# Feed-forward products in two-by-two blocks with seven products for eight, in a decoder layer on one core

## The chip, the core and the metric

The kernel runs on one core of a Trainium2 chip, as one launch. The metric is the device time of that launch in microseconds (us). The engines are PE (TensorE: matmuls and the loads of their stationary operand), DVE (VectorE), ACT (ScalarE), POOL (GpSimd) and SP (SyncE, which here only issues DMAs). Matmuls write to PSUM; all other data is in SBUF, 128 partitions wide.

## What is computed

One layer over 528 tokens (512 of the input behind 16 learned ones), model width 1024, hidden width 2816, all in float32:

```python
def swiglu_ffn(h, w_gu, w_down):
    gate, up = jnp.split(h @ w_gu, 2, axis=-1)
    return (jax.nn.silu(gate) * up) @ w_down

h = h + 0.5 * swiglu_ffn(rms_norm(h, ffn1_norm), ffn1_w_gu, ffn1_w_down)
h = h + hybrid_mixer(rms_norm(h, mix_norm), w_in, conv_w, b_f, ...)
h = h + 0.5 * swiglu_ffn(rms_norm(h, ffn2_norm), ffn2_w_gu, ffn2_w_down)
return rms_norm(h[:, 16:], final_norm)
```

The mixer (a short gated convolution beside an attention with forget gates) is the same in both kernels. The two feed-forward networks hold most of the arithmetic: 1024 x 5632 weights for gate and up, 2816 x 1024 for down, each.

## The kernel before

Activations lie transposed, with features on partitions and tokens as columns: hT is 8 tiles of [128, 528]. A weight tile of 128 x 128 is the stationary operand of a matmul and the tokens are the moving one. To keep float32's precision at float32r's speed, each operand is split into two float32r parts, hi and lo, and each product is made of three matmuls: hi x hi, hi x lo, lo x hi (mm, L281). Splitting costs one ACT cast for hi (L78) and one DVE subtraction for lo (L79).

The class Weights streams the weights in the order of use: SP loads run two loads ahead (L57), and units of [128, 8, 128] are split three units ahead. The first network works in chunks of 8, 8 and 6 of the 22 hidden tiles of 128. For each hidden tile the gate product runs over 8 tiles of the model width, then the up product, then ACT and DVE make silu(gate) x up and split it into hid_h and hid_l (gate, L299 to L306; up, L312 to L319). After each chunk the down products of the 8 output tiles run over the chunk's hidden tiles and DVE adds them to hT (L322). Its 528 columns are two matmuls of 264 in two PSUM banks. The second network does the same with 512 columns in one bank, chunks of 8, 8 and 4, and a last chunk of 2 whose down product has the tokens on partitions, so that the final norm can begin per tile of tokens. The gain of the norm is on the operand (L239, L244), and 1/rms is multiplied onto the product.

The start is written out by hand: the first three products of the first network run side by side while the input arrives, tile by tile. Elsewhere a scheduler sets the order of the instructions on each engine, and Weights.done and take place the splits between the products. POOL does some memsets, the sums of squares at the start (L254) and the small DMAs of the attention's forget gates (L544, L553).

Of the kernel before, what the change touches and what calls it, by code (L numbers as in the profile page):

```python
# [14 lines left out]
P = 128  # L15
D = 1024
# [17 lines left out]
class Weights:  # L34
    """Streams weight units [128, k, 128]: loads run ahead, then each unit is split
    into two float32r parts hi + lo, which together hold every bit of the float32."""

    def __init__(self, nc, raw_pool, pool, ahead, loads_ahead):
        self.nc, self.raw_pool, self.pool = nc, raw_pool, pool
        self.ahead, self.loads_ahead = ahead, loads_ahead  # L40
        self.loads, self.units = [], []
        self.raw, self.ready = {}, {}
        self.n_loaded = self.n_ready = self.n_used = 0
# [8 lines left out]
    def load(self, whole=True):  # L52
        ap, nk, cols = self.loads[self.n_loaded]
        t = self.raw_pool.tile([P, 2048], F32, name="raw")
        v = t[:, : nk * cols].rearrange("p (k c) -> p k c", c=cols)
        if whole:
            self.nc.sync.dma_start(out=v, in_=ap)  # L57
# [6 lines left out]
    def open(self, pool=None):  # L64
        """Takes the next unit's two tiles; split_slice fills them."""
        pool = pool or self.pool
        hi = pool.tile([P, 8, P], F32R, name="w_hi")
        lo = pool.tile([P, 8, P], F32R, name="w_lo")
# [11 lines left out]

    def split(self):
        load, _, nk, cols = self.units[self.n_ready]
        while self.n_loaded < len(self.loads) and self.n_loaded <= load + self.loads_ahead:
            self.load()
# [10 lines left out]
    def take(self, i=0):  # L95
        self.fill()
        return self.ready[self.n_used + i]

    def done(self):
        del self.ready[self.n_used]  # L100
        self.n_used += 1
        self.fill()


class Acc:
    """A product in PSUM: in one bank, or in the halves of its columns in two banks.
    Columns are named by position (0..L)."""
# [6 lines left out]
    def each(self, f):  # L114
        """f(psum view, g) for as few views as hold the product; g cuts an operand alike."""
# [9 lines left out]
def layer(ctx, tc, x, meta, n1, gu1, dn1, nm, w_in, conv_w, b_f, g_conv, g_attn, w_out, n2, gu2, dn2, nf, out):  # L125
# [751 lines left out]
```

## Time and profile before

| | us |
|---|---|
| three runs, median | 1015.25 |
| lowest, highest | 1014.94, 1017.09 |
| span of the profiled execution | 1013.3 |
| PE busy | 998.2 |
| DVE busy | 516.9 |
| ACT busy | 382.1 |
| POOL busy | 43.0 |

The span is from the first to the last instruction; what the runs' time has beyond it lies around the program. The page gives busy time by engine, then the chain of work that ended last, followed back from the last instruction to what released each step. Groups of instructions are named by line, engine, operation and tiles (out<-in). Matmuls are pipelined, so the duration of one is longer than the distance between two starts. The first network lasts until about 401 us, the mixer until about 641, the second network until about 993, and the rest is the final norm and the output.

### The profile page before, as it was taken

The page shows a single profiled execution, that of the slowest core. Times are in us where ns is not written, and L with a number is a line of the kernel's source. Part 1 is how long each engine was busy: PE and PEld are TensorE (multiplying, and loading weights), DVE is VectorE, ACT ScalarE, POOL GpSimd, SP SyncE. Part 2 cuts the span into 40 slices and gives each one's busy share as a digit, 9 for nine tenths or more (in the row PEclk, how much of TensorE's full clock was granted, in tenths as well). Part 3 has the DMA queues.
Part 4 walks back from the last instruction along what each step waited for, and adds up shares of the span by engine and source line. Part 5 has one row for each costly group of instructions (what it writes and reads, how often), then busy time and mean ns, then how long its engine had stood idle before and what let it go on. Part 6 is the DMA issues. An engine that isn't in the chain of part 4 may idle for free.

```text
span 1013.3 us, 14940 instructions
## 1 busy us (share of the span) xinstructions
PE 998.2 (99%) x6338; PEld 906.6 (89%) x6338; DVE 516.9 (51%) x787; ACT 382.1 (38%) x612; POOL 43.0 (4%) x76
## 2 busy tenths in 40 slices
PE   9999999999999999999999999999999999999996
PEld 8999999999999999989899888888888888888884
DVE  6844333444334446676766657644433444334445
ACT  5622212222122244675656665523222232222335
POOL 4100000000000002200000000100000000000002
PEclk9999999999999999999999999999999999999998
DMA  6422222223223212232233122323332223231312
GB/s 211 160 91 84 84 83 84 83 84 126 83 84 93 86 53 72 77 104 66 63 83 95 58 83 84 104 94 114 102 105 83 83 84 125 84 104 41 107 40 84
DMA packets 102707, 91.99 MB, mean 91 GB/s; under 512 B 3604, under 2 KB 101056, under 8 KB 102640
## 3 DMA queue, kind: packets, MB, share of 16 engines
q1 hardware_dynamic: 101792, 90.42, 28.4%
q8 instruction: 50, 0.82, 0.4%
q10 hardware_dynamic: 144, 0.52, 0.1%
q0 software_dynamic: 704, 0.09, 0.1%
q14 instruction: 17, 0.14, 0.0%
HBM read 88.86 MB, written 2.10 MB: 90 GB/s over the span
## 4 chain that ended last, share of the span: by engine, by line
PE 92%; ACT 3%; DVE 3%; issue 1%; DMA 0%; SPq 0%; DVEq 0%; ACTq 0%
PE bank L281 50%; PE acc L281 37%; PE bank L712 2%; PE bank L679 1%; PE bank L643 1%; DVE w_lo L79 1%; ACT w_hi L78 0%; DVE sm L650 0%; DMA raw<-in_ffn_w_gu_dram 0%; ACT sm L153 0%; DVE hT L389 0%; PE bank L514 0%; ACT sm L664 0%; ACT xh L239 0%; PE bank L802 0%
## 5 line engine op out<-in xcount | busy, mean ns | idle before, releaser
L78 ACT CAST w_hi<-raw 128x1024 fp32r<-128x1024 f32 (+5 forms) x184 | 175.5, 958 | 550.5 <-PE bank L281 218.3
L79 DVE TENSOR_TENSOR w_lo<-raw,w_hi 128x1024 fp32r<-128x1024 f32 (+4 forms) x183 | 208.2, 1141 | 43.6 <-ACT w_hi L78 40.3
L281 PE MATMUL bank<-xl,w_hi 128*128 128x512 f32 (+2 forms) x672 | 216.1, 353 | 0.0
L281 PE MATMUL bank<-xh,w_hi 128*128 128x512 f32 (+2 forms) x672 | 216.1, 352 | 0.0
L281 PE MATMUL bank<-xh,w_lo 128*128 128x512 f32 (+2 forms) x672 | 215.4, 352 | 0.0
L281 PE MATMUL acc<-xh,w_hi 128*128 128x264 f32 x704 | 141.7, 286 | 1.7 <-ACT xh L239 1.3
L281 PE MATMUL acc<-xh,w_lo 128*128 128x264 f32 x704 | 142.0, 287 | 0.0
L281 PE MATMUL acc<-xl,w_hi 128*128 128x264 f32 x704 | 140.6, 284 | 0.3 <-DVE xl L244 0.3
L281 PEld LDWEIGHTS bank<-xh,w_hi 128*128 128x128 f32 x672 | 118.1, 188 | 18.8
L281 PEld LDWEIGHTS bank<-xh,w_lo 128*128 128x128 f32 x672 | 117.9, 188 | 17.8
L281 PEld LDWEIGHTS bank<-xl,w_hi 128*128 128x128 f32 x672 | 117.7, 188 | 17.8
L281 PEld LDWEIGHTS acc<-xh,w_hi 128*128 128x128 f32 x704 | 109.5, 190 | 2.2 <-ACT xh L239 1.6
L281 PEld LDWEIGHTS acc<-xh,w_lo 128*128 128x128 f32 x704 | 109.0, 190 | 0.0
L281 PEld LDWEIGHTS acc<-xl,w_hi 128*128 128x128 f32 x704 | 107.6, 188 | 0.5 <-DVE xl L244 0.5
L281 PE MATMUL acc<-hid_h,w_hi 128*128 128x264 f32 x352 | 71.7, 285 | 0.0
L281 PE MATMUL acc<-hid_l,w_hi 128*128 128x264 f32 x352 | 71.7, 285 | 0.0
L281 PE MATMUL acc<-hid_h,w_lo 128*128 128x264 f32 x352 | 71.6, 285 | 0.0
L281 PE MATMUL bank<-hid_h,w_hi 128*128 128x512 f32 x160 | 62.9, 393 | 0.0
L281 PE MATMUL bank<-hid_h,w_lo 128*128 128x512 f32 x160 | 62.4, 390 | 0.0
L281 PE MATMUL bank<-hid_l,w_hi 128*128 128x512 f32 x160 | 62.4, 390 | 0.0
L281 PEld LDWEIGHTS acc<-hid_h,w_hi 128*128 128x128 f32 x352 | 54.7, 188 | 0.0
L281 PEld LDWEIGHTS acc<-hid_l,w_hi 128*128 128x128 f32 x352 | 54.5, 188 | 0.0
(233 smaller groups left out, 1061.7 us busy)
## 6 DMA issues: line engine op xcount, KB each, us to landing
raw<-in_ffn_w_gu_dram SPq DMA_DIRECT2D x42, 1024.0 KB, 5.0
raw<-in_ffn_w_down_dram SPq DMA_DIRECT2D x16, 1024.0 KB, 5.2
raw<-in_w_in_dram SPq DMA_DIRECT2D x24, 512.0 KB, 4.0
raw<-in_ffn_w_down_dram SPq DMA_DIRECT2D x4, 768.0 KB, 4.6
raw<-in_ffn_w_down_dram SPq DMA_DIRECT2D x6, 512.0 KB, 3.7
raw<-in_w_out_dram SPq DMA_DIRECT2D x3, 896.0 KB, 5.1
raw<-in_ffn_w_gu_dram SPq DMA_DIRECT2D x8, 256.0 KB, 6.4
out_dram<-ob SPq DMA_DIRECT2D x8, 256.0 KB, 2.2
```

Source lines behind the costliest of these rows:

```text
L78: nc.scalar.copy(h, src)
L79: nc.vector.tensor_sub(lw, src, h.bitcast(F32))
L281: nc.tensor.matmul(ap, lhsT=wt[:, kw, :], rhs=mt[:, k, c0 - off:c1 - off], start=(first and a == 0 and b == 0), stop=(last and a == len(ks ...
L643: nc.tensor.matmul(t[:, o:o + c1 - c0], lhsT=qt[:, i * P:(i + 1) * P], rhs=kt[:, c0:c1], start=(b == 0), stop=(b == 1))
L679: nc.tensor.transpose(o, sm[:, SOFF[i] + j * P:SOFF[i] + (j + 1) * P], ident)
L712: nc.tensor.matmul(oo, lhsT=lt, rhs=rt, start=(a == 0 and n_ == 0), stop=(a == 1 and n_ == len(ops) - 1))
```

## The change

The products of both networks are cut into blocks of two by two by two: two tiles of the output (gate and up of one hidden tile, or two output tiles of down), pairs of tiles of the inner dimension, and two halves of the token columns (264 each in the first network, 256 in the second). With blocks A of the weights and B of the activations, the seven products are A11 B11, A12 B21, and five of sums of blocks, in Winograd's form of Strassen's scheme. A unit of seven products runs over 4 pairs of inner tiles for gate and up, and over 3 or 2 pairs of hidden tiles for down. Gate and up of the first 6 hidden tiles of the first network and the first 4 of the second stay as they were ("classical"), and so does the down product of the last 2 hidden tiles of the second network.

The activations of each pair of tiles are kept in seven forms, each split into hi and lo: three are blocks and four are sums of blocks, which POOL makes (L379 to L386). They lie in one arena of float32r with the operands of the mixer. Of the four sums of weight blocks, two are made by a DMA that POOL issues and that adds to what SP has loaded before (L474, L478), two by DVE (L486, L489). Each of the four groups of weights (nat, s24, ss, 22) is then cast by ACT (L499) and subtracted by DVE (L503). Where several outputs share a partial result, ACT copies it from one bank to the next with its sign turned (L546, L547), and a fifth bank holds the one product that two outputs take from SBUF.

Work in the networks is now placed by hand in slots, one product each: Slots.at puts a task behind slot t, on whatever engine it runs. `b` is a unit's first slot; the next unit's is b + 7.

```diff
+        def pair_forms(self, r, s0, s1, t0, t1):
...
+            def sums1():
+                t = ts["t"]
+                b12, b21, b22 = self.half(s0(), 1), self.half(s1(), 0), self.half(s1(), 1)
+                nc.gpsimd.tensor_add(t[:, 1], t[:, 0], b22)
+                nc.gpsimd.tensor_sub(t[:, 2], b12, b22)
+                nc.gpsimd.tensor_sub(t[:, 3], b21, t[:, 1])
...
+        def prep(self, b, nat, base, acc, a22, nj):
+            def load():
+                raw["nat"] = self.pool_raw.tile([P, 8, P], F32, name="raw")
+                nc.sync.dma_start(out=raw["nat"][:, :2 * nj], in_=nat)
+                raw["ss"] = self.pool.tile([P, 2, nj, P], F32, name="ss", tag="ss", bufs=2)
+                for i in range(2):
+                    nc.sync.dma_start(out=raw["ss"][:, i], in_=base[i])
+            def add():
+                for i in range(2):
+                    nc.gpsimd.dma_start(out=raw["ss"][:, i], in_=acc[i], accum_op=ALU.add)
+            def s2():
+                raw["s24"] = self.pool.tile([P, 2, nj, P], F32, name="s24")
+                nc.vector.tensor_add(raw["s24"][:, 0], raw["ss"][:, 1], raw["nat"][:, 0:2 * nj:2])
+            def s4():
+                nc.vector.tensor_add(raw["s24"][:, 1], raw["s24"][:, 0], raw["nat"][:, 1:2 * nj:2])
...
+            sl.at(b - 13, load, 3)
+            sl.at(b - 9, add, 3)
+            sl.at(b - 7, load22, 3)
+            sl.at(b - 4, s2, 3)
+            sl.at(b - 3, s4, 3)
+            for nm_, t in (("nat", b - 3), ("s24", b - 1), ("ss", b), ("22", b + 2)):
+                sl.at(t, lambda nm_=nm_: hi(nm_), 3)
+                sl.at(t + 1, lambda nm_=nm_: lo(nm_), 3)
...
+        def products(self, nj, rhs, w):
+            b = sl.slot(prod(A, "nat", lambda j: 2 * j, F_B11, True))
+            sl.slot(self.p4)
+            sl.slot(prod(A, "nat", lambda j: 2 * j + 1, F_B21, False))
+            sl.slot(prod(B, "s24", lambda j: j, F_T2, False))
+            sl.slot(prod(E, "ss", lambda j: nj + j, F_T1, True))
+            sl.slot(prod(B, "ss", lambda j: j, F_T3, False))
+            sl.slot(prod(C, "s24", lambda j: nj + j, F_B22, False))
+            self.p4 = prod(B, "22", lambda j: j, F_T4, False)
...
+            sl.at(b + 1, lambda: nc.scalar.activation(B, A, AF.Copy, scale=-1.0), 0)
+            sl.at(b + 4, lambda: nc.scalar.activation(C, B, AF.Copy, scale=-1.0), 0)
+            sl.at(b + 5, copy_e, 0)
...
+        def down(self, j0, nj, m):
+            sl.at(b + 3, add(h00, A), 0)
+            sl.at(b + 6, add(h11, B), 0)
+            sl.at(b + 6, lambda: nc.gpsimd.tensor_sub(h11, h11, self.e5), 0)
+            sl.at(b + 7, add(h01, C), 0)
+            sl.at(b + 7, lambda: nc.gpsimd.tensor_add(h01, h01, self.e5), 0)
+            sl.at(b + 9, add(h10, B), 0)
...
+            g_units(range(14, NF))
+            for m in range(0, ND, 2):
+                F.down(6, 2, m)
+            for m in range(0, ND, 2):
+                for i, t in enumerate(F.down(8, 3, m)):
+                    def fin(d=m + i):
+                        operand(d, GMIX, L, xm)
+                        squares(d, L, nc.gpsimd)
+                    sl.at(t, fin, 1)
```

In the first network down runs over hidden pairs 0 to 2, 3 to 5, 6 and 7, and 8 to 10; in the second over 0 to 2, 3 to 5, 6 and 7, and 8 and 9. The gain, 1/rms and the half of the residual are now on the forms of the operand and on the hidden tiles, and the output is finished in hT in place of a buffer of its own.

DVE in the first network, one hidden tile, before (w_lo is a weight's low part, s and hd the gate and the product with up):

```order
L299 SCALAR_TENSOR_TENSOR s<-acc,rs 128x528
L79 TENSOR_TENSOR w_lo<-raw,w_hi 128x1024
L306 SCALAR_TENSOR_TENSOR s<-s,rs 128x528
L312 TENSOR_TENSOR hd<-acc,s 128x528
L79 TENSOR_TENSOR w_lo<-raw,w_hi 128x1024
L319 TENSOR_TENSOR hid_l<-hd,hid_h 128x528
```

The same engine and place now (s_1814 and s_1941 are sums of weight blocks, e_1845 the shared product, r_1765 the block A22):

```order
L489 TENSOR_TENSOR s_1814<-s_1814,raw 128x512
L503 TENSOR_TENSOR w_lo<-raw,w_hi 128x1024
L572 TENSOR_TENSOR hd<-acc,e_1845 128x264
L575 TENSOR_TENSOR s<-acc,e_1845 128x264
L503 TENSOR_TENSOR w_lo<-s_1814,w_hi 128x1024
L503 TENSOR_TENSOR w_lo<-ss,w_hi 128x1024
L579 SCALAR_TENSOR_TENSOR hd<-acc,s 128x264
L580 SCALAR_TENSOR_TENSOR hd<-hd,s 128x264
L503 TENSOR_TENSOR w_lo<-r_1765,w_hi 128x512
L486 TENSOR_TENSOR s_1941<-ss,raw 128x512
L371 TENSOR_TENSOR arena<-hd,arena 128x264
```

A hidden tile has four low parts in place of two, two sums of weights, and the next unit's first sum stands between this unit's evacuations and the forms of its hidden tile.

POOL from the start's sums of squares through the whole first network to the mixer, before:

```order
L378 AFFINE_SELECT mask<-mask 128x128
L254 TENSOR_TENSOR ssum<-ssum,sq 128x528 x7
L87 MEMSET w_hi 128x1024
L493 MEMSET q2a 64x512
L493 MEMSET k2a 64x528
```

POOL within the down units of the second group of hidden pairs now (ss receives the accumulating DMAs, e_2604 and e_2707 are shared products):

```order
L478 DMA ss<-in_ffn_w_down_dram 128x3x128 x2
L384 TENSOR_TENSOR ts<-ts,hd 128x264
L385 TENSOR_TENSOR ts<-hd 128x264
L386 TENSOR_TENSOR ts<-hd,ts 128x264
L478 DMA ss<-in_ffn_w_down_dram 128x3x128 x2
L606 TENSOR_TENSOR hT<-hT,e_2604 128x264
L608 TENSOR_TENSOR hT<-hT,e_2604 128x264
L478 DMA ss<-in_ffn_w_down_dram 128x3x128 x2
L606 TENSOR_TENSOR hT<-hT,e_2707 128x264
L608 TENSOR_TENSOR hT<-hT,e_2707 128x264
```

Where POOL had nothing between the sums of squares and the memset of the mixer's first weights, it now has two accumulating DMAs per unit, and the forms' sums or two corrections of hT stand between one pair and the next.

ACT where the start hands over to the third hidden tile of the first network, before (y and tt are steps of 1/rms):

```order
L153 ACTIVATE y_492<-y_492 128x264
L145 ACT_TABLE_LOAD
L260 ACTIVATE tt<-y_492 128x264
L153 ACTIVATE raw<-raw 128x528 x2
L317 CAST hid_h<-raw 128x528
L78 CAST w_hi<-raw 128x1024
```

And now:

```order
L191 ACTIVATE y_482<-y_482 128x264
L183 ACT_TABLE_LOAD
L294 ACTIVATE tt<-y_482 128x264
L455 CAST w_hi<-raw 128x1024
L191 ACTIVATE raw<-raw 128x528 x2
L455 CAST w_hi<-raw 128x1024
```

The first cast that stands here now is that of the third hidden tile's own gate weights; before, these were cast ahead of the steps of 1/rms, and the one shown is for a later tile.

## Rows read from the trace of the kernel before

**Rows 1.** The page: busy time by engine, and the last chain's shares by engine.

```profile
PE 998.2 (99%) x6338; PEld 906.6 (89%) x6338; DVE 516.9 (51%) x787; ACT 382.1 (38%) x612; POOL 43.0 (4%) x76
...
PE 92%; ACT 3%; DVE 3%; issue 1%; DMA 0%; SPq 0%; DVEq 0%; ACTq 0%
```

**Rows 2.** The chain in order of time: start us, us, what; the two networks.

```profile
38.24 362.72 PE acc L281 x2976
...
641.37 308.94 PE bank L281 x1341
```

**Rows 3.** Busy time by stretch: PE, PEld, DVE, ACT, POOL, clock, DMA share, GB/s.

```profile
38.20:401.00 362.80, 362.80 (x2978) 362.79 (x2978) 157.76 (x190) 99.22 (x125) 1.12 (x2) 1.00 0.28 88
...
500.00:600.00 100.00, 98.58 (x637) 89.37 (x636) 68.33 (x155) 61.70 (x123) 3.57 (x10) 1.00 0.25 76
...
641.00:950.00 309.00, 309.00 (x1343) 251.80 (x1342) 132.73 (x156) 82.03 (x101) 2.20 (x1) 1.00 0.28 92
```

**Rows 4.** Timeline of PE (start us, us): 258 columns, then 512.

```profile
476.22 0.40 PE L281 MATMUL bank<-xh,w_hi 128*128 128x258 f32 x2
...
476.94 0.28 PE L281 MATMUL bank<-xh,w_hi 128*128 128x258 f32 x1
...
699.81 0.40 PE L281 MATMUL bank<-xl,w_hi 128*128 128x512 f32 x1
...
710.93 0.40 PE L281 MATMUL bank<-xl,w_hi 128*128 128x512 f32 x1
```

**Rows 5.** Groups by form: busy us, mean ns | idle before them, releasers.

```profile
L79 DVE TENSOR_TENSOR w_lo<-raw,w_hi 128x1024 fp32r<-128x1024 f32 x145 | 177.6, 1225 | 37.0 <-ACT w_hi L78 33.9 <-PE bank L281 0.6
...
L78 ACT CAST w_hi<-raw 128x1024 fp32r<-128x1024 f32 x145 | 152.1, 1051 | 494.4 <-PE bank L281 194.0 <-PE acc L281 170.1 <-issue 127.2
...
L244 DVE SCALAR_TENSOR_TENSOR xl<-hT,gains,xh 128x528 fp32r<-128x528 f32 x16 | 12.2, 766 | 4.7 <-ACT xh L239 4.6
...
L79 DVE TENSOR_TENSOR w_lo<-raw,w_hi 128x768 fp32r<-128x768 f32 x8 | 7.7, 959 | 0.0
...
L79 DVE TENSOR_TENSOR w_lo<-raw,w_hi 128x512 fp32r<-128x512 f32 x8 | 5.4, 681 | 0.0
...
L695 DVE TENSOR_TENSOR l<-bank,h 128x384 fp32r<-128x384 f32 x8 | 4.4, 549 | 0.0
...
L551 DVE SCALAR_TENSOR_TENSOR ks<-bank,rs 128x264 f32<-128x264 f32 x8 | 3.3, 424 | 0.4 <-PE bank L281 0.4
```

**Rows 6.** DVE beside POOL: two timeline rows, then line 79 and two groups.

```profile
21.38 1.31 POOL L254 TENSOR_TENSOR ssum<-ssum,sq 128x528 f32<-128x528 f32 x1 [0.87 <-ACT sq L253]
...
21.56 1.41 DVE L79 TENSOR_TENSOR w_lo<-raw,w_hi 128x256 fp32r<-128x256 f32 x1
...
L79 DVE TENSOR_TENSOR w_lo<-raw,w_hi x22: 407/696/1553, 6.5 to 56.8; 128x256 fp32r<-128x256 f32 x16, 128x1024 fp32r<-128x1024 f32 x6
...
L79 DVE TENSOR_TENSOR w_lo<-raw,w_hi 128x256 fp32r<-128x256 f32 x16 | 11.0, 713 | 0.1
...
L254 POOL TENSOR_TENSOR ssum<-ssum,sq 128x528 f32<-128x528 f32 x7 | 9.5, 1357 | 16.4 <-ACT sq L253 16.3
```

**Rows 7.** DMA issues (KB, us to landing), a POOL issue, an SP issue.

```profile
raw<-in_ffn_w_down_dram SPq DMA_DIRECT2D x6, 512.0 KB, 3.7
...
xc<-in_x_dram SPq DMA_DIRECT2D x2, 256.0 KB, 3.2
...
bf<-in_b_f_dram POOLq DMA_DIRECT2D x1, 0.0 KB, 4.8
...
L544 POOL DMA_DIRECT2D q2a<-fr x4 | 2.2, 554 | 20.8 <-DVE fr L536 16.1 <-PE bank L643 4.7
...
204.39 0.37 SPq L57 DMA_DIRECT2D raw<-in_ffn_w_gu_dram  x1
```

**Rows 8.** Timeline of DVE where the start hands over to the network.

```profile
34.42 2.36 DVE L79 TENSOR_TENSOR w_lo<-raw,w_hi 128x1024 fp32r<-128x1024 f32 x2 [0.24 <-ACT w_hi L78]
...
39.23 0.43 DVE L261 SCALAR_TENSOR_TENSOR tt<-sm,tt 128x264 f32<-128x264 f32 x1 [0.76 <-ACT tt L260]
```

More of the change, by code (lines that the diff above doesn't have):

```diff
@@ L321, in down @@
[L321 to L340 removed]
+    F_B11, F_B21, F_B22, F_T1, F_T2, F_T3, F_T4 = range(7)
@@ L443, in layer @@
             nc.vector.tensor_copy(gains[:, 8:], gp[:, :36])
+            nc.vector.tensor_scalar(ghalf, gains[:, :24], -0.5, None, ALU.mult)
             table(SILU_SET)
-        with tc.tile_pool(name="hid1", bufs=2, reuse_waits="tile") as hid1:
-            for ci, (_, nf_) in enumerate(CHUNKS1):
-                hh, hl = hidden(hid1, L)
-                gate_up(new1, nf_, hh, hl, 0, start=[*accs, a3] if ci == 0 else None)
-                for m in range(ND):
-                    acc = new1()
-                    mm(acc, W.take(), range(nf_), hh, hl)
-                    down(acc, m)
-                    if ci == len(CHUNKS1) - 1:
-                        operand(m, GMIX, L)
-                        squares(m, L)
-                    W.done()
+        for _ in range(4):
+            W.done(False)
@@ L515, in layer @@
         sa = new(L)
[L516 removed]
+        row_sums(sa, *split2(ssum, L))
         W.done()
@@ new lines, in tokens, with gain_row @@
+                nc.scalar.copy(hT[:, m, NM:], bank_x)
+            done = []
+            for m in range(0, ND, 2):
+                done += F.down(8, 2, m)
+            g_units(range(NF - N_LAST, NF))
+            F.end()
+            for m, t in enumerate(done):
+                sl.add(t + 2, lambda m=m: tokens(m))
+            t_gb = done[0]
+            def gain_row():
+                v["gb"] = pool.tile([P, 4, 256], F32, name="ts").rearrange("p a c -> p (a c)")
+                nc.scalar.dma_start(out=v["gb"], in_=nf.rearrange("(o d) -> o d", o=1).broadcast_to([P, D]))
@@ new lines, in layer, with obs @@
+            W.done(False)
+            for k in range(NF - N_LAST, NF):
+                add_row(dn2, k)
+            sl.at(n - 16, W.prefetch, 4)
+            for i in range(N_LAST):
+                sl.at(n - 4 + 3 * i, W.split, 4)
+            sl.run()
+        table(EXP_SET)
+        hh, hlo = hl
+        gb = v["gb"]
+        ws = [W.take(i) for i in range(N_LAST)]
+        pss = bk[0] + bk[2] + [bank_x, bank_e] + bk[1]
+        def obs(i, b):
+            return hT[:, 4 * b:4 * b + 4, NM + i * P:NM + (i + 1) * P]
```

593 lines of the change are left out of this document (406 added, 187 removed).

## Prediction, made before the changed kernel ran

> **What bounds the kernel now.** I read the page first: PE is busy 99% of the span, and the chain that ended last runs on PE for 92% of it [rows 1]. The chain in order of time then shows where: one unbroken piece of 362.72 us in the first feed-forward network and one of 308.94 us in the second [rows 2]. In the same two stretches DVE is busy 157.76 of 362.80 us (43%) and 132.73 of 309 us (43%), ACT 27%, POOL hardly, the DMA engines 28%, and the granted clock is full [rows 3]. So PE alone sets the time there, and fewer matmul columns shorten the kernel as long as nobody else becomes late. The profiled execution has a span of 1013.3 us; the median of the runs is 1015.25, so 1.95 us lie around the span, and I keep them.
>
> **What PE saves.** A matmul of 264 columns takes 0.1219 us of the unbroken piece (362.72 / 2976 [rows 2]). One of 512 columns starts every 0.2317 us (48 between 699.81 and 710.93 [rows 4]). The change cuts the first network from 3168 to 2844 matmuls of 264 columns: 324 x 0.1219 = 39.5 us. In the second network 1344 matmuls of 512 columns (18 gate/up tiles x 48, 480 in the down products) become 2352 of 256. Nearest to 256 columns are the 258-column ones of the mixer: six starts in 0.72 us, 0.120 each [rows 4]; the line through 264 and 512 columns gives 0.118. I take 0.119: 1344 x 0.2317 - 2352 x 0.119 = 311.4 - 279.9 = 31.5 us (33.4 at 0.118, 29.2 at 0.120). Together 71.0 us.
>
> The Trainium skill ("TensorE: Matmul & The Clock Gate", Back-to-back issue gap) gives 262 cycles for 256 columns at full clock, which is 0.109 us. The rows at 258 and 264 columns lie 0.01 us above its formula, and those at 512 by 0.016; by that page of the Trainium skill the second network would save another 23 us, and as the rows contradict it I give this no chance.
>
> **What the other engines get instead.** The two networks now hold 66 units of seven products: 34 gate/up units (84 matmuls, 10.2 us of PE in the first network), 20 down units over three pairs of hidden tiles (63, 7.7 us) and 12 over two pairs (42; 5.12 us in the first network, 5.00 in the second). Each unit splits four groups of weights (1024, 1024, 1024 and 512 columns in a gate/up unit, where before it was two of 1024 for the same tile), adds two sums on DVE, and has four evacuations at half width. DVE by the rows [rows 5]: gate/up 3 x 1.225 + 0.681 for the low parts, 2 x 0.681 for the sums, 4 x 0.424 for the evacuations, and about 1.2 for half a pair of hidden forms: 8.6 of 10.2 us. Down with three pairs: 3 x 0.959 + 0.549 + 2 x 0.549 + 4 x 0.424 = 6.2 of 7.7. Down with two pairs: 3 x 0.681 + 0.41 + 2 x 0.41 + 4 x 0.424 = 5.0 of 5.0 to 5.1. ACT has less in every unit (a cast of 1024 columns is 1.05 us [rows 5], about 6.8 of 10.2 in a gate/up unit). So DVE goes from 43% to 85% and, in the short units, to 100%.
>
> **POOL beside DVE.** POOL now adds the forms and two corrections of hT in each down unit. The trace shows what that does: at 21.56 a DVE instruction of 256 columns with both inputs in SBUF, which takes 0.407 us undisturbed, took 1.41 and ended just after POOL's addition that had started at 21.38 [rows 6]. Over 16 such instructions the mean is 0.713, so 16 x 0.306 = 4.9 us were lost beside 9.5 us of POOL additions: 0.52 us for each us of POOL. A POOL addition of 264 columns is half of 1.357 [rows 6], 0.68 us. Gate/up and three-pair units hide the loss (0.7 us each). The last four down units of the first network don't: they also make the mixer's operand and the squares, DVE 6.2 + 2 x 0.766 (0.77 by the row of the 528-column operand [rows 5]) = 7.75, beside POOL's 2 x 0.68 + 2 x 1.36 = 4.07, of which 2.1 are lost: 9.9 against 7.7, **8.8 us** for the four; between 0 and 16 us with none or all of POOL's time lost.
>
> **The accumulating DMAs.** Two of the sums per unit are made by DMAs that POOL issues and that add to SBUF. No row of before shows one. On SP the loads of ss wait until DVE is through with the unit before last; on POOL the accumulating pair waits for these loads, and the forms and hT corrections are queued behind it; on DVE the sum (L486) waits for the pair, and behind it stand the low parts and the evacuations that PE's next product needs. With two ss buffers this is a loop over two units: two SP issues (0.37 each [rows 7], 0.8 with their gaps), the landing of the plain loads, the accumulating pair (call it A, from POOL's turn to landing), and DVE's work from L486 to the low part of ss. For two-pair units: 0.8 + 3.2 (256 KB [rows 7]) + A + 3.7 (0.41 x 2 + 0.68 x 3 + 0.42 x 2), per unit (7.7 + A) / 2. Three pairs: (0.8 + 3.7 + A + 4.8) / 2. Gate/up: (0.8 + 3.7 + A + 6) / 2. A is bounded below by a plain load of the same bytes with one POOL issue, 3.2 + 0.55 [rows 7], and above by twice a 512 KB load plus the slowest landing of a POOL DMA, 2 x 3.7 + 4.8 = 12.2. I take 5, near the lower rows because the transfers are small: two-pair units 6.35 us, 1.23 too long four times and 1.35 eight times, **15.7 us**. Three-pair (7.15) and gate/up (7.75) units hide it. DVE's own excess in the short units (5.0 + 0.7 - 5.05) lies inside this. At A = 3.75 it is 8 us. As to bandwidth: 76 GB/s of mostly 512-byte rows took 25% of the DMA engines in the mixer [rows 3]; a gate/up unit moves 1.83 MB in 10.2 us, 180 GB/s, which is 59%, or 76% if an accumulated byte costs double.
>
> The Trainium skill ("DMA: Bandwidth & Descriptors", Anatomy of one DMA) puts a DMA from this queue at 2.0 us plus its bytes over 436 GB/s. An estimate from that page of the Trainium skill is 2.6 us for the pair of a short unit, by which the term of 15.7 would be about 1 and the forecast some 15 us lower; no run here shows it yet.
>
> **Smaller terms.** At the start of the first network before's weights for the third tile are split at 34.42, ahead of the norm; now the cast stands behind the table load and the last square (ACT's order in the section on the change), whose end DVE waited for at 39.23 [rows 8]. Cast 1.05 and low part 1.225 then end at 41.5, while PE is through at 38.24 [rows 2]: **3 us**. At the handover to the mixer the last two operand tiles come after the last product (evacuation 0.42, then ACT's and DVE's halves of the operand, 0.77 each [rows 5]), while the mixer's first product can start on the earlier ones: 0 to 6 us, I take **3**. Waits of in-order queues at 85% DVE load, one or two products of slack each: 0 to 25 us, I take **5**; no row gives it. The tail (final norm) keeps its work: nothing.
>
> **Sum.** 1015.25 - 71.0 + 8.8 + 15.7 + 3 + 3 + 5 = 979.8. I predict **980**. With the small terms at their ends it is 955 to 1010.
>
> **The rivals.** *All hidden.* POOL's additions fall where DVE waits for PE, A is at its lower end: only the start and handover remain, 1015.25 - 71 + 6 = 950, up to 960. For it: DVE's work in the units, 34 x 8.6 + 20 x 6.2 + 12 x 5.0 = 476 us, fits into PE's 556. The page of the Trainium skill on DMAs, named above, would give it such an A. Against it: the short units, where DVE has no slack. *Accumulation bounds (slower).* The loop above, with A long: A = 8 gives 2.8 x 12 in the short units and 1.1 x 20 in the three-pair units, 56 us in place of 15.7, so about 1020. From A of about 7.75 the change loses; at the upper bound A = 12.2 the units come to 9.95, 10.75 and 11.35 us, 59 + 63 + 42 = 164 us, time about 1128. For it: 256 to 512 rows per DMA to be issued by POOL, where the row shows 2 at 0.55 us [rows 7]; each accumulated row has to be read on both sides. Against it: the DMA engines stand idle two thirds of the time. *It does not do what it says*: the order of PE's instructions holds 2268 and 2352 matmuls of 264 and 256 columns in the units, so the cut of 71 us is there; I give it nothing. A time within 0.2% (about what a measurement here can tell from no change) needs A between 7.6 and 7.9: a narrow strip.
>
> The Trainium skill speaks for the second rival: "Collectives: The Full Stack" (Part 3) says that an accumulating transfer reads two sources and runs at half the rate of a copy. As a mechanism here that doubles a 512 KB landing to 7.4 us and a short unit's 256 KB to 6.4; with 0.55 of issue A is 7 in the short units and 8 in the others, 28 + 21 us in place of 15.7, and the time about 1013.
>
> **How the numbers follow.** All hidden 0.20; the forecast, 960 to 1008, 0.50; between that and no change 0.07; within 0.2% 0.03; accumulation or DVE as the bound beyond that 0.20. Faster 0.77, same 0.03, slower 0.20. For 8 in 10 the range takes in the lower case from 948 (0.05 below it) and of the slow one as far as A = 8.5 or so, 1030 (0.13 above).
>
> **What would show it.** PE: 0.119 us between starts of 256 columns, clock still full. DVE busy about 85% in the networks; additions with two SBUF inputs stretched beside POOL's. L486 waiting for the accumulating DMAs in the two-pair down units and hardly in gate/up units; PE idle there and in the last four down units of the first network. If L486 waits in every unit, the slow rival is right; if PE is unbroken, the first. Wrong would be the whole sum if PE waited mostly for ACT's copies in PSUM, which I cost at nothing: one product (0.73 us in a short unit) covers a copy of 0.4.

## The result, and the profile after

The changed kernel takes 1066.94 us (median of four, 1065.74 to 1067.87) against 1015.1: a ratio of 1.0507, 95% interval 1.0492 to 1.0522. It is 52 us slower where 35 us faster was forecast, and it lies above the whole range. The profiled execution has a span of 1066.2 us against 1013.3, so 52.9 us have to be found.

The page of the changed kernel, the lines that answer to [rows 1]: busy time by engine, and the last chain by engine.

```profile
PE 974.7 (91%) x7022; PEld 921.5 (86%) x7022; DVE 798.4 (75%) x1236; ACT 576.4 (54%) x1037; POOL 413.0 (39%) x395
...
PE 58%; DVE 14%; DMA 11%; issue 7%; ACT 5%; POOL 4%; SPq 0%; ACTq 0%; POOLq 0%; DVEq 0%
```

PE is busy for 23.5 us less (974.7 against 998.2) and idle for 76.4 us more (1066.2 - 974.7 = 91.5 against 15.1); that is the 52.9. The chain ran on PE for 92% of the span; now it is 58%, and DVE, the DMAs and POOL hold 29%.

Busy time by stretch, as in [rows 3] (PE, PEld, DVE, ACT, POOL, clock, DMA share, GB/s): the first network, then the second.

```profile
38.20:430.00 391.80, 349.68 (x2646) 337.99 (x2647) 304.76 (x411) 196.28 (x333) 194.17 (x171) 0.96 0.67 137
...
680.00:1044.00 364.00, 333.35 (x2518) 319.64 (x2519) 283.11 (x404) 190.32 (x331) 178.25 (x156) 0.97 0.71 147
```

DVE went from 43% to 78% in both networks, the DMA engines from 28% to about 70%, and the granted clock is no longer full: 0.96 and 0.97 in place of 1.00. Over the whole span its mean is 0.973, before 0.997. A clock that is at the lower of its two levels (1.2 of 2.4 GHz) for a share s of the span has the mean 1 - s/2, so by an estimate from these two means (1 - 0.973) x 1066.2 = 28.8 us were lost to it now, and 3.0 before. But both figures count a last stretch at the lower level that stands behind PE's last matmul and costs PE nothing; in the changed kernel it is this one:

```profile
1059.00:1066.20 7.20, 0.00 (x0) 0.00 (x0) 1.77 (x4) 1.55 (x4) 0.00 (x0) 0.50 0.68 195
```

Half of its 7.2 us, 3.6, goes off the 28.8; before, the last 5.7 us are such a stretch, and half of them, 2.9, goes off the 3.0. So about 25 us were lost now and nothing before. Not all of it need be in the time: the granted clocks of the four runs of the changed kernel lie between 0.973 and 0.981, 8.5 us apart by this estimate, and their times only 2.1.

Who PE waited for in the changed kernel (engine, line and tile, then us in total, times, the longest):

```profile
PE bank L529 <- DVE w_lo L503: 17.7, 12, 3.6
PE acc L529 <- ACT acc L546: 15.7, 32, 1.3
PE acc L529 <- DVE hT L602: 12.2, 12, 2.4
PE acc L529 <- DVE w_lo L503: 8.7, 6, 3.5
PE bank L316 <- DVE w_lo L459: 5.5, 4, 2.3
PE bank L316 <- ACT w_hi L455: 5.3, 1, 5.3
PE acc L316 <- DVE w_lo L459: 3.8, 4, 2.0
PE bank L316 <- DVE arena L278: 2.3, 1, 2.3
```

These eight rows are 71 us, and they have three causes. The waits for ACT's copy L546 and DVE's addition L602 stand only in the first network (27.9 us; acc is its PSUM tile). Those for the low parts L503 stand in both (26.4). Those for L455 and L459 are the classical tiles (14.6). The last row is the handover to the mixer.

The matmuls themselves do what was forecast. PE in the second network, six starts apart:

```profile
848.72 0.28 PE L529 MATMUL bank<-arena,w_lo 128*128 128x256 f32 x1
...
849.44 0.28 PE L529 MATMUL bank<-arena,w_lo 128*128 128x256 f32 x1
```

0.72 us for six is 0.120 each, so the columns saved are worth 39.5 + (311.4 - 2352 x 0.120) = 68.7 us.

### The profile page after: what moved, and what is told of

It is laid out like the page before. It is cut to its first block, busy times and chain, and to the rows that moved or that the text cites. A ratio compares the mean times of both kernels' runs of the same rounds, so it can differ in the third digit from the quotient of the medians.

```text
span 1066.2 us, 18472 instructions
## 1 busy us (share of the span) xinstructions
PE 974.7 (91%) x7022; PEld 921.5 (86%) x7022; DVE 798.4 (75%) x1236; ACT 576.4 (54%) x1037; POOL 413.0 (39%) x395
## 4 chain that ended last, share of the span: by engine, by line
PE 58%; DVE 14%; DMA 11%; issue 7%; ACT 5%; POOL 4%; SPq 0%; ACTq 0%; POOLq 0%; DVEq 0%
PE bank L529 16%; PE acc L529 16%; PE bank L316 16%; DMA ss<-in_ffn_w_gu_dram 5%; DMA ss<-in_ffn_w_down_dram 5%; DVE w_lo L503 4%; PE sm L529 3%; PE acc L316 2%; PE bank L1052 2%; DVE arena L371 1%; DVE s L486 1%; DMA raw<-in_ffn_w_gu_dram 1%; POOL ss L478 1%; DVE w_lo L80 1%; ACT arena L273 1%
## 5 line engine op out<-in xcount | busy, mean ns | idle before, releaser
L529 PE MATMUL bank<-arena,w_hi 128*128 128x256 f32 x1568 | 289.4, 287 | 1.6 <-ACT bank L547 0.9
L529 PE MATMUL acc<-arena,w_hi 128*128 128x264 f32 x1296 | 251.5, 293 | 28.0 <-ACT acc L546 15.7
L529 PEld LDWEIGHTS bank<-arena,w_hi 128*128 128x128 f32 x1568 | 247.8, 194 | 3.3 <-ACT bank L547 1.5
L529 PE MATMUL bank<-arena,w_lo 128*128 128x256 f32 x784 | 226.2, 289 | 17.8 <-DVE w_lo L503 17.7
L529 PEld LDWEIGHTS acc<-arena,w_hi 128*128 128x128 f32 x1296 | 206.0, 194 | 37.4 <-ACT acc L546 22.6
L316 PE MATMUL bank<-arena,w_hi 128*128 128x512 f32 (+2 forms) x896 | 205.5, 334 | 7.6 <-ACT w_hi L455 5.3
L529 PE MATMUL acc<-arena,w_lo 128*128 128x264 f32 x648 | 188.1, 290 | 8.7 <-DVE w_lo L503 8.7
L529 PEld LDWEIGHTS bank<-arena,w_lo 128*128 128x128 f32 x784 | 152.4, 194 | 21.3 <-DVE w_lo L503 21.1
L316 PEld LDWEIGHTS bank<-arena,w_hi 128*128 128x128 f32 x896 | 143.2, 190 | 24.1 <-ACT w_hi L455 5.8
L316 PE MATMUL bank<-arena,w_lo 128*128 128x512 f32 (+2 forms) x448 | 128.4, 333 | 5.5 <-DVE w_lo L459 5.5
L478 POOL DMA_DIRECT2D ss<-in_ffn_w_gu_dram x68 | 89.5, 1551 | 92.0 <-DVE s L489 35.7
L478 POOL DMA_DIRECT2D ss<-in_ffn_w_down_dram x64 | 82.8, 1517 | 56.5 <-DVE w_lo L503 19.2
L486 DVE TENSOR_TENSOR s<-ss,raw 128x512 f32<-128x512 f32 (+2 forms) x66 | 49.2, 745 | 62.0 <-issue 47.6
L499 ACT CAST w_hi<-s 128x1024 fp32r<-128x1024 f32 (+2 forms) x66 | 59.9, 907 | 64.0 <-DVE s L489 38.0
L316 PEld LDWEIGHTS bank<-arena,w_lo 128*128 128x128 f32 x448 | 76.2, 190 | 15.6 <-DVE w_lo L459 7.9
L503 DVE TENSOR_TENSOR w_lo<-s,w_hi 128x1024 fp32r<-128x1024 f32 (+2 forms) x66 | 87.5, 1325 | 0.4 <-ACT w_hi L499 0.4
L503 DVE TENSOR_TENSOR w_lo<-ss,w_hi 128x1024 fp32r<-128x1024 f32 (+2 forms) x66 | 86.4, 1309 | 0.0
L503 DVE TENSOR_TENSOR w_lo<-raw,w_hi 128x1024 fp32r<-128x1024 f32 (+2 forms) x66 | 69.8, 1058 | 14.4 <-ACT w_hi L499 14.3
L80 DVE TENSOR_TENSOR w_lo<-raw,w_hi 128x1024 fp32r<-128x1024 f32 (+2 forms) x53 | 56.5, 1076 | 20.3 <-ACT w_hi L79 19.9
L316 PE MATMUL acc<-arena,w_hi 128*128 128x264 f32 x384 | 65.0, 296 | 3.3 <-ACT w_hi L455 1.7
```

The costliest lines, as they stand in the source:

```text
L80: nc.vector.tensor_sub(lw, src, h.bitcast(F32))
L316: nc.tensor.matmul(ap, lhsT=wt[:, kw, :], rhs=mt[:, k, c0 - off:c1 - off], start=(first and a == 0 and b == 0), stop=(last and a == len(ks ...
L478: nc.gpsimd.dma_start(out=raw["ss"][:, i], in_=acc[i], accum_op=ALU.add)
L486: nc.vector.tensor_add(raw["s24"][:, 0], raw["ss"][:, 1], raw["nat"][:, 0:2 * nj:2])
L499: nc.scalar.copy(w[nm_][0][:, :m], src(nm_))
L503: nc.vector.tensor_sub(w[nm_][1][:, :m], src(nm_), w[nm_][0][:, :m].bitcast(F32))
```

## The experiments

All times are beside runs of the kernel before on the same chip, whose median stayed between 1015.7 and 1016.0. The first four kernels are the changed kernel with one edit. Of the second to the fifth one run each is given. These four and the last kernel leave a part of the sums out: their times tell what that part costs, and they are not faster kernels.

**One tile for each PSUM bank.** In the first network a PSUM tile had two banks, used in turn by units; in the second each bank is a tile. ACT's copy in both (us, duration, engine; what it waited for):

```profile
284.19 0.28 PE L529 MATMUL acc<-arena,w_lo 128*128 128x264 f32 x1
...
284.51 0.38 ACT L546 ACTIVATE acc<-acc 128x264 f32<-128x264 f32 x1 [1.67 <-PE acc L529]
...
284.94 0.39 PE L529 MATMUL acc<-arena,w_hi 128*128 128x264 f32 x1 [0.47 <-ACT acc L546]
...
824.83 0.37 ACT L546 ACTIVATE bank<-bank 128x256 f32<-128x256 f32 x1 [0.20 <-PE bank L529]
```

In the first network the copy from A to B starts at 284.51, when the product that stands between (the last one of the unit before, which writes the other bank of the same tile) has just ended, though A was done a product earlier. PE's next product needs A again, and so it starts at 284.94, 0.75 us after the matmul before it in place of 0.12. In the second network the copy does not wait so, and PE waits for it only once, 0.5 us.

```diff
-    with tc.tile_pool(name="ps1", bufs=3, space=PSUM) as ps1, tc.tile_pool(name="ps1s", bufs=2, space=PSUM) as ps1s:
+    with tc.tile_pool(name="ps1", bufs=6, space=PSUM) as ps1, tc.tile_pool(name="ps1s", bufs=2, space=PSUM) as ps1s:
...
-            t = ps1.tile([P, 2, 512], F32, name="acc")
-            return Acc([t[:, 0], t[:, 1]], L, both=t), t
+            t = [ps1.tile([P, 512], F32, name="acc") for _ in range(2)]
+            return Acc(t, L), t
...
```

> One edit: in the first network each PSUM bank is a tile of its own (six tiles of one bank in place of three of two). Theory PSUM tiles: the changed kernel's PE waits for ACT's copies at L546 (32 times, 21 us with the restart) and for DVE's additions to hT at L602 (12 times, 14 us) only because both halves of a two-bank tile count as one, so both vanish: 1067 - 35 = 1032, a few us less where the clock no longer falls. Rival, the next wait takes their place (weights' low parts, late by the accumulating DMAs or by DVE): the copies' waits go but waits for L503 grow in the first network, 1055 or more.

Measured: 1052.89, ratio 1.0354 (1.0328 to 1.038), 14 us less than the changed kernel. PE's waits, the same list:

```profile
PE acc L529 <- DVE w_lo L503: 19.3, 14, 4.9
PE bank L529 <- DVE w_lo L503: 19.3, 13, 3.9
...
PE sm L529 <- DVE w_lo L503: 3.7, 4, 1.6
...
PE acc L529 <- ACT acc L546: 1.7, 2, 1.3
```

Both theories hold in part. The copy's wait fell from 15.7 to 1.7 us and that for L602 from 12.2 to 1.1, as the tile theory says. But the waits for L503 rose from 26.4 to 42.3: more than half of the 25 us that were freed was taken by what stood behind.

**The accumulating DMAs left out, or made plain.**

```diff
-            sl.at(b - 9, add, 3)
```

> The accumulating DMAs of all 66 units are left out (the sums ss then hold one block only), nothing else. Theory accumulation loop: the 18 waits of PE for low parts at L503 (29.5 us with the restart) and a part of the half-clock stretches vanish, 1067 - 35 = about 1032 (1025 to 1040), and DVE no longer stands at L486. Rival, DVE itself is late because POOL's additions stretch its instructions: waits at L503 stay, over 1050.

Measured: 1028.08, 39 us less; DVE is idle 0.0 us ahead of the sum, where it was 62, PE's waits for L503 fell from 26.4 to 5.3 us and the granted clock rose to 0.987.

```diff
-                    nc.gpsimd.dma_start(out=raw["ss"][:, i], in_=acc[i], accum_op=ALU.add)
+                    nc.gpsimd.dma_start(out=raw["ss"][:, i], in_=acc[i])
```

> The same POOL DMAs with the same bytes, order and waits, but they overwrite in place of adding (the sums ss then hold one block only). If adding itself is what takes long (landing 4.3 to 6.2 us against 2.5 to 4.2 of SP's loads of the same size), landing falls to about 4 us and most of the gain of leaving them out comes: 1040. If it is the issue by POOL (1.3 us each) and its queue, the time stays within 8 us of 1067.

Measured: 1041.64, 25 of the 39 us. The DMAs of POOL in the changed kernel (KB, us to landing), and the group of its issues (busy, mean ns):

```profile
ss<-in_ffn_w_gu_dram POOLq DMA_DIRECT2D x68, 256.0 KB, 6.2
...
ss<-in_ffn_w_down_dram POOLq DMA_DIRECT2D x40, 192.0 KB, 5.5
...
ss<-in_ffn_w_down_dram POOLq DMA_DIRECT2D x24, 128.0 KB, 4.3
...
L478 POOL DMA_DIRECT2D ss<-in_ffn_w_gu_dram x68 | 89.5, 1551 | 92.0 <-DVE s L489 35.7 <-DMA ss<-in_ffn_w_gu_dram 19.3 <-ACT e L544 16.0
```

The same four with plain writes:

```profile
ss<-in_ffn_w_gu_dram POOLq DMA_DIRECT2D x68, 256.0 KB, 3.9
...
ss<-in_ffn_w_down_dram POOLq DMA_DIRECT2D x40, 192.0 KB, 3.9
...
ss<-in_ffn_w_down_dram POOLq DMA_DIRECT2D x24, 128.0 KB, 3.0
...
L478 POOL DMA_DIRECT2D ss<-in_ffn_w_gu_dram x68 | 51.7, 762 | 88.0 <-DMA ss<-in_ffn_w_gu_dram 37.2 <-DVE s L489 36.9 <-ACT arena L370 5.4
```

The same bytes land after 3.9, 3.9 and 3.0 us in place of 6.2, 5.5 and 4.3, and one issue takes 0.76 us on POOL in place of 1.55. So adding is most of what costs, and it does so at both ends, in POOL's issue and in the transfer. The Trainium skill ("Collectives: The Full Stack", Part 3) has the reduce step of a ring collective, which reads two sources, at half the rate of a copy; it says so of collectives, not of a single DMA into SBUF. The landing here is 1.4 to 1.6 times as long, and it holds a part that does not grow with the bytes (plain, 256 KB land after 3.9 us and 128 KB after 3.0), so this case neither shows the half rate nor speaks against it.

**POOL's corrections left out.** DVE and POOL in a down unit of the second network, in the changed kernel:

```profile
887.61 0.95 DVE L503 TENSOR_TENSOR w_lo<-raw,w_hi 128x768 fp32r<-128x768 f32 x1
...
889.14 3.13 DVE L503 TENSOR_TENSOR w_lo<-s,w_hi 128x768 fp32r<-128x768 f32 x1
...
889.62 1.83 POOL L606 TENSOR_TENSOR hT<-hT,e 128x256 f32<-128x256 f32 x1
...
890.32 2.52 POOL L608 TENSOR_TENSOR hT<-hT,e 128x256 f32<-128x256 f32 x1
```

A low part of 768 columns takes 0.95 us at 887.61 and 3.13 at 889.14, where POOL makes its two corrections; these take 1.83 and 2.52, where the shortest of their line takes 0.73. The Trainium skill ("SBUF — State Buffer", SBUF: two separate sides) says that a DVE instruction with two SBUF inputs and a POOL instruction that reads SBUF lock each other out for a whole instruction; these rows agree in that both sides are stretched, and cannot show whether one stood still for a whole instruction of the other.

```diff
-            sl.at(b + 6, lambda: nc.gpsimd.tensor_sub(h11, h11, self.e5), 0)
...
-            sl.at(b + 7, lambda: nc.gpsimd.tensor_add(h01, h01, self.e5), 0)
```

> POOL's two corrections of hT in each of the 32 down units (L606, L608) are left out (their addend is missing from the result). Theory contention: DVE's low parts in the down units, 2 to 3 us beside a correction in place of 0.95, go back to 0.95, and waits of PE for L503 in the down units and just behind go: 1067 - 20 = 1047. Rival, the accumulation loop alone sets these waits: L503 waits stay, within 6 us of 1067.

Measured: 1065.57, 1 us less, which is no more than the changed kernel's own runs differ by. PE's waits for L503 did not fall, they rose (34.6 us), and DVE's idle time ahead of the sum rose from 62 to 95 us. As long as the sum from the DMA comes late, DVE has time for POOL.

**Single banks and no DMAs together.**

> Both at once: one tile for each PSUM bank in the first network, and the accumulating DMAs left out (the sums ss hold one block only). The single bank edit took 35 us of waits and gave 18 back as waits at L503; the DMAs alone took 39 us. If the two are one behind the other (what the banks gave back was the accumulation loop), together they give 35 + 39 and the clock's part, 1067 - 75 = 992, 985 to 1000. If both hide a third bound (DVE's work), the sum stays at 1010 or more.

Measured: 1004.24, 63 us less than the changed kernel. With the DMAs out of the way the banks are worth 24 us (1028.08 to 1004.24) and not 14, but the sum stays 12 short of the expectation: waits for L503 come back in part (10.8 us), now with DVE not idle at all ahead of the sum, and the classical tiles still wait 14.

**The sums on POOL.** This version has the single banks, loads one block in place of four and lets POOL add.

```diff
...
-                for i in range(2):
-                    nc.gpsimd.dma_start(out=raw["ss"][:, i], in_=acc[i], accum_op=ALU.add)
+                nc.gpsimd.tensor_add(raw["ss"][:, 0], raw["nat"][:, 0:2 * nj:2], raw["ss"][:, 1])
...
+                nc.gpsimd.tensor_add(raw["ss"][:, 1], raw["ss"][:, 1], raw["22"])
...
```

> On top of the single banks the accumulating DMAs are replaced and the result is the full one: of the four blocks that SP loaded and POOL's DMAs added, only A21 is loaded; POOL adds A11 (in nat) to it, and A22 (r22, now two buffers, loaded earlier) to a second one; e5 has one buffer. POOL's work per gate/up unit: two additions of 512 columns, 1.36 each undisturbed, in place of two DMA issues of 1.55. Accumulation theory: the waits at L503 go except those of a busy DVE, near the kernel with the DMAs left out: 1000, 990 to 1012. Contention theory: POOL's additions stretch DVE's low parts by half a us for each us, 34 x 1.4 + 20 x 1.05 + 12 x 0.7 = 77 us of DVE, which the gate/up units (1.6 of slack) hold and the short ones do not: 1015 to 1035.

Measured: 1040.91, ratio 1.0251 (1.0226 to 1.0276), a little beyond what contention was to give: 12 us less than with the single banks alone, and 37 more than with the DMAs left out. A low part of DVE in the changed kernel:

```profile
L503 DVE TENSOR_TENSOR w_lo<-raw,w_hi 128x1024 fp32r<-128x1024 f32 x34 | 42.5, 1251 | 5.5 <-ACT w_hi L499 5.4
```

The same with POOL's sums, one of these, and DVE's wait for it:

```profile
L504 DVE TENSOR_TENSOR w_lo<-raw,w_hi 128x1024 fp32r<-128x1024 f32 x34 | 63.9, 1878 | 2.7 <-ACT w_hi L500 2.7
...
L479 POOL TENSOR_TENSOR ss<-ss,r 128x512 f32<-128x512 f32 x34 | 61.8, 1819 | 6.9 <-DMA r<-in_ffn_w_gu_dram 4.6
...
DVE s L487 <- POOL ss L479: 29.4, 29, 2.2
```

The low part rose from 1.251 to 1.878 us, 21 us over the 34 units, and POOL's addition of 512 columns takes 1.82. DVE's busy time is 58.7 us longer than with the single banks alone (850.8 against 792.1). Made by DVE itself, the sums would take 2 x (34 x 0.681 + 20 x 0.549 + 12 x 0.41) = 78 us, by an estimate from instructions of the same sizes [rows 5]. So handing them to POOL saved DVE about a quarter. The stretching is not all that costs here: DVE also waits 29.4 us for the second of POOL's sums, and no run tells the two apart.

**Classical weights a product earlier**, on top of that.

```diff
-            self.sl.at(t - 8, load, 3)
-            self.sl.at(t - 2, hi, 3)
-            self.sl.at(t - 1, lambda: nc.vector.tensor_sub(w["w"][1], w["r"], w["w"][0].bitcast(F32)), 3)
+            self.sl.at(t - 12, load, 3)
+            self.sl.at(t - 6, hi, 3)
+            self.sl.at(t - 5, lambda: nc.vector.tensor_sub(w["w"][1], w["r"], w["w"][0].bitcast(F32)), 3)
```

> The kernel with POOL's sums, with one further edit: the weights of the classical tiles are loaded, cast and subtracted one product (four slots) earlier. Theory in-order queues: PE's waits at L455 and L459 (16.7 us in the changed kernel, since ACT's cast stands behind the cast of sums that POOL still makes) mostly vanish, 14 us less than the kernel without this edit. Rival, the engines are simply full there: the waits move to later tiles, less than 5 us.

Measured: 1034.02, 7 us less, half of the expectation. The waits for L459 fell from 8.9 to 2.2 us, the one of 5.3 us for L455 stayed. ACT ahead of it, in the changed kernel:

```profile
705.50 1.05 ACT L370 CAST arena<-ts 128x1024 fp32r<-128x1024 f32 x1 [6.32 <-POOL ts L386]
...
709.10 0.41 ACT L370 CAST arena<-xn 128x256 fp32r<-128x256 f32 x1 [2.02 <-DVE xn L403]
...
710.28 1.04 ACT L455 CAST w_hi<-raw 128x1024 fp32r<-128x1024 f32 x1
```

The cast of the weights (710.28) stands behind a cast of sums that waits 6.32 us for POOL, and behind one that waits 2.02 us for DVE. DVE's and POOL's rows show for whom POOL waits:

```profile
701.23 1.21 DVE L371 TENSOR_TENSOR arena<-ts,arena 128x1024 fp32r<-128x1024 f32 x1
...
702.52 0.74 POOL L379 TENSOR_TENSOR ts<-xn 128x256 f32<-128x256 f32 x1 [4.43 <-DVE arena L371]
```

POOL waits for DVE to have read the sums before (until 702.44; their tile has one buffer), DVE comes to them only when ACT has cast them and its own earlier work is done, and ACT's next cast is behind POOL again. Earlier weights did not open this ring.

**Three ss buffers.** If the latency of the DMA pair is what costs and not its work, the pair has only to start earlier. SBUF had no room for a third buffer in the first network until hidden tiles 2 and 3 moved to the pool tmp.

```diff
-                raw["ss"] = self.pool.tile([P, 2, nj, P], F32, name="ss", tag="ss", bufs=2)
+
+            def load_ss():
+                raw["ss"] = self.pool.tile([P, 2, nj, P], F32, name="ss", tag="ss", bufs=3)
...
+            sl.at(b - 19, load_ss, 3)
...
-            sl.at(b - 9, add, 3)
+            sl.at(b - 14, add, 3)
...
-                t = F.classical(f, accB, accC, x1, hd_pool=pool if f < 4 else None)
+                t = F.classical(f, accB, accC, x1, hd_pool=None)
```

> Full computation, accumulating DMAs as in the changed kernel, single banks as in the first experiment, and one further edit: three ss buffers in place of two, loads of ss issued 19 slots ahead of a unit in place of 13 and the accumulating pair 14 ahead in place of 9, so that they have ten slots until DVE needs the sum in place of five (room in SBUF: hidden tiles 2 and 3 of the first network move to the pool tmp). Loop theory: what costs is the latency of the pair, not its work; so nearly the time with the pair left out, 1004 + 5 = 1009 (1004 to 1018). Rival: the POOL queue and the DMA engines are the limit (POOL's issues of 1.55, 1.25 MB a unit that count double), then the waits at L503 stay as with single banks alone, 1040 or more.

Measured: 1008.44, ratio 0.9935 (0.9914 to 0.9956), faster than the kernel before, and 44 us less than with single banks alone. The DMAs take no less time (in gate/up units 6.3 us to landing, 1.55 per issue), and DVE no longer waits for them. Its idle time ahead of the sum, 62 us in the changed kernel, is the last figure here:

```profile
L488 DVE TENSOR_TENSOR s<-ss,raw 128x512 f32<-128x512 f32 (+2 forms) x66 | 57.0, 863 | 0.1
```

Of PE's waits for the low parts 11.0 us are left. So it was the pair's latency that cost, and not its work. The third buffer and the earlier places were not tried apart. In the changed kernel SP's own loads of ss already waited for DVE's L503, 107.0 us in 30 waits, which speaks for the buffer and does not prove it.

> The same with the classical tiles' weights split four slots earlier, which took 7 us from the kernel with POOL's sums: 7 us less than the kernel with three buffers, about 1002, and below the kernel before. Rival: with the hidden tiles in the pool tmp the engines wait for buffers there, no gain.

Measured: 1004.54, ratio 0.9889 (0.9874 to 0.9904), 4 us less.

**The mixer's operand later.** The last four down units of the first network in that kernel, ACT and then DVE:

```profile
369.46 0.74 ACT L273 ACTIVATE arena<-hT,gains 128x528 fp32r<-128x528 f32 x1 [1.12 <-POOL hT L611]
...
370.64 0.50 ACT L501 CAST w_hi<-r 128x384 fp32r<-128x384 f32 x1
...
370.23 0.77 DVE L278 SCALAR_TENSOR_TENSOR arena<-hT,gains,arena 128x528 fp32r<-128x528 f32 x1 [1.42 <-ACT arena L273]
370.92 2.08 DVE L505 TENSOR_TENSOR w_lo<-ss,w_hi 128x768 fp32r<-128x768 f32 x1
```

ACT's operand cast waits for POOL's correction, the weights' cast for the next product stands behind it (370.64), DVE waits for ACT, and its low part then falls beside POOL's next addition.

```diff
-                    sl.at(t, fin, 1)
+                    sl.at(t + 3, fin, 4)
```

> The previous kernel (single banks, three ss buffers, classical weights earlier) with one edit in the last four down units of the first network: the mixer's operand and the squares of an output tile are issued three slots later and behind the weights' tasks of their slot. There, 12.5 us of PE's waits stand, with ACT's operand cast waiting for POOL's correction of hT and DVE's low part behind it. In-order theory: the casts and low parts of the next unit go ahead, 5 to 9 us of the waits go, 1004.5 - 6 = 998. Contention theory (POOL's corrections and squares stretch DVE's low parts to 2 us): less than 3 us.

Measured: 997.4, ratio 0.9827 (0.9805 to 0.9849), 7 us less. PE's waits in this stretch (343 to about 401 us) fell from 10.7 to 5.1 us. This is the fastest kernel with the full result, 18.6 us below the kernel before.

> As the kernel with the later operand, and the classical tiles' casts and low parts stand first in their slot. A wait of 5.3 us for L455 in the second network, behind two casts of forms that wait for DVE and POOL, shrinks by 3 us, and the clock does not fall there: 4 us less than the kernel without it, 994. Rival: the forms of the operand are then later and the first Strassen unit waits for them, no gain.

Measured: 999.9 (0.9834 to 0.9872): no gain. The wait for L455 fell from 5.4 to 2.0 us, and those for L459 and for the first unit's cast took its place, much as the rival says, though it is for the cast of its weights and not for the forms that the first unit waits.

> The fastest kernel so far (single banks, three ss buffers, classical weights earlier, the mixer's operand later; 997.4) with POOL's two corrections of hT in each down unit left out (their addend is missing from the result). Left out of the changed kernel itself they were worth 1 us, while the accumulation loop set the time. Contention theory: with the loop gone DVE, stretched beside the corrections, is the next bound in the short and the last down units: 6 to 12 us less, 985 to 991. Rival: PE still covers it, less than 3 us.

Measured: 990.74, ratio 0.9755 (0.9738 to 0.9771), 6.7 us less, at the lower edge of what contention was to give. The low parts of the three-pair units with the corrections, and without:

```profile
L505 DVE TENSOR_TENSOR w_lo<-ss,w_hi 128x768 fp32r<-128x768 f32 x20 | 27.3, 1365 | 0.0
```

```profile
L505 DVE TENSOR_TENSOR w_lo<-ss,w_hi 128x768 fp32r<-128x768 f32 x20 | 19.0, 950 | 0.0
```

So the same edit is worth 1 us at most in the changed kernel and 6.7 here: POOL's corrections were a real bound with another one standing in front of it. How much of the 6.7 is DVE's stretched low parts and how much POOL's shorter queue, no run separates.

## Why the prediction was wrong, step by step

| Term of the sum | forecast | measured |
|---|---|---|
| PE's columns | -71.0 | -68.7 |
| copies and evacuations in PSUM | 0 | 27.9 idle |
| accumulating DMAs | 15.7 | 26.4 idle; 39 when left out, 44 from the third buffer after the single banks |
| POOL beside DVE | 8.8 (last four down units) | the corrections of all 32 down units: 1 here; 6.7 once the rest is gone |
| waits of in-order queues | 5 | 14.6 idle (classical tiles) |
| start, handover | 3, 3 | 1.7, 2.3 idle |
| clock | 0 | about 25 (estimate from the mean clocks) |

**What PE saves** was right. 256 columns start every 0.120 us, the upper of the three values considered, and 264 as before.

**The copies in PSUM** were the first failed step. The prediction costed them at nothing, since one product covers a copy of 0.4 us, and named PE waiting for them as what would make the sum wrong. The cover was there in time but not in order: with two banks in one tile the copy waits for that very product. A wait costs more than its idle time: 0.47 us in the rows at 284, and 0.63 from start to start (0.75 in place of 0.12). It returned 32 times, and with one tile for each bank it went. The order of waits was there to be read before the run; I read the durations only.

**The accumulating DMAs** were the second: the latency of the loop was the right mechanism, with a wrong size and the wrong places. A was taken as 5 us. By the rows of the result, one issue of 1.55 and the landing after the next issue make it 7.8 in a gate/up unit, 7.0 with three pairs and 5.8 with two. Put into the loops of the prediction, that gives (9.3 + 7.0) / 2 = 8.2 against 7.7 in 20 units and (7.7 + 5.8) / 2 = 6.8 against 5.1 in 12, some 30 us, and 26.4 were measured. The row taken as the lower bound, a plain load, was the wrong neighbour: adding doubles the issue and lengthens the landing by about half. Of the two other estimates of A in the prediction, 2.6 us for a short unit is less than half of the 5.8, and 7 and 8 us lie near the measured 5.8 to 7.8. That 30 and 26.4 lie so close is partly luck, for the places differ. DVE's sums in the changed kernel, for gate/up, three-pair and two-pair units (behind the second bar the idle time before them, and what ended it):

```profile
L486 DVE TENSOR_TENSOR s<-ss,raw 128x512 f32<-128x512 f32 x34 | 27.8, 818 | 41.7 <-issue 29.9 <-DMA ss<-in_ffn_w_gu_dram 6.5 <-DVE w_lo L503 5.1
...
L486 DVE TENSOR_TENSOR s<-ss,raw 128x384 f32<-128x384 f32 x20 | 14.2, 708 | 13.8 <-issue 11.6 <-DVE w_lo L503 2.0
...
L486 DVE TENSOR_TENSOR s<-ss,raw 128x256 f32<-128x256 f32 x12 | 7.2, 602 | 6.6 <-issue 6.1 <-DVE w_lo L503 0.3 <-DMA ss<-in_ffn_w_down_dram 0.2
```

Two thirds of the idle time stand in gate/up units, where the prediction had hardly any. Of PE's 26.4 us, each wait counted to the unit whose sum DVE had made last, 8.4 fall to gate/up, 8.9 to three-pair and 9.2 to two-pair units, where the loops give nothing, 10 and 20. Why gate/up units wait, for which the loop has time to spare, stays open. The kernel with three buffers shows that the latency, and not the work, was the price.

**POOL beside DVE** is there and about as strong as forecast. Leaving out POOL's 64 corrections, 46.7 us at their shortest 0.73, took 38.9 us of DVE's busy time from the changed kernel (798.4 to 759.5) and 23.0 from the kernel with the later operand (800.6 to 777.6): 0.83 and 0.49 us for each us of POOL, where 0.52 was taken. But it is worth 1 us behind the loop and 6.7 without it.

**The in-order queues** were given 5 us without a row. The classical tiles cost 14.6, since before the splits ran three units ahead and now two slots ahead, behind the forms in ACT's queue.

**The clock** was no term at all. It was full in the kernel before as long as PE had work, with 15.1 us of idle time in the whole span. PE in the changed kernel around one wait, then the stretch behind it (busy times and clock, as above):

```profile
359.23 0.80 PE L529 MATMUL acc<-arena,w_hi 128*128 128x264 f32 x2 [1.20 <-DVE hT L602]
359.83 0.42 PE L529 MATMUL acc<-arena,w_lo 128*128 128x264 f32 x1
...
360.49 0.42 PE L529 MATMUL acc<-arena,w_lo 128*128 128x264 f32 x1
...
363.06 0.41 PE L529 MATMUL acc<-arena,w_hi 128*128 128x264 f32 x2
...
363.67 0.28 PE L529 MATMUL acc<-arena,w_lo 128*128 128x264 f32 x1
...
359.83:360.50 0.67, 0.67 (x5) 0.67 (x5) 0.35 (x2) 0.00 (x0) 0.00 (x0) 0.50 0.60 169
```

Three matmuls take 0.66 us from 359.83 to 360.49, 0.22 each, with a granted clock of 0.50, and five take 0.61 from 363.06, 0.122 each. Each matmul of the stretch behind the wait costs 0.1 us more. Idle time in a PE that had hardly any was paid for a second time here, in the matmuls behind it.

**The sum.** Idle time 76.4, the clock about 25, and 78 more waits than before (86 against 8) at 0.16 beyond their idle time, 12 by an estimate from the one wait at 284, less 68.7: some 45 of the 52.9 us. Some 8 us are not attributed.

**The rivals.** The slow one, accumulation as the bound, came nearest: it is the largest single cause (39 us when left out). But its A, 5.8 to 7.8 as measured, reaches the 7.75 from which it loses only in gate/up units, and alone it would have given about 1003 (979.8 - 15.7 + 39). So it did not decide against the change by itself; the waits in PSUM, the classical tiles and the clock, which no rival held, were added to it. The chances were too high for faster because the terms were taken as the only ones: two of 25 to 28 us each were left out, and the in-order queues had 5 for 14.6.

## What to carry to other kernels

When the busy engine is to lose its cover, read each new wait in the order of instructions and ask what it waits for by tile, not what it takes: here two halves of one tile waited for each other. Where a loop over two buffers has a latency of more than two units, try a third buffer and an earlier start before making its work cheaper; here that took 44 us. Do not count on relieving DVE by handing POOL a sum of two SBUF operands: here DVE saved a quarter of it. And where one edit returns less than its waits, try it again after the next bound is gone: the banks were worth 14 and then 24 us, the corrections 1 and then 7.

## What the runs showed of the hardware that was not expected

- A POOL issue of an accumulating DMA of 256 KB took 1.55 us, of a plain one 0.76, and the landing 6.2 against 3.9.
- POOL's additions and DVE's instructions on SBUF stretched each other: 0.95 to 3.13 us on DVE beside 0.73 to 1.83 and 2.52 on POOL. With POOL's two corrections left out the low parts of 768 columns were back at 0.95 in the mean.
- Behind four waits of PE between 350 and 360, 3.0 us together and none above 1.2, the granted clock was 0.50 (from 359.83 to 360.50), and matmuls of 264 columns started every 0.22 us in place of 0.122.
